# A layer of gated DeltaNet and neighbourhood attention on one core: the attention's values read from the normed values without a copy, one lasting slot for the wide weights, value stores issued by ScalarE, and one norm segment in another bank

## The chip, the cores and the metric

The kernel runs on one core of a Trainium2 chip. The core has a matrix engine (TensorE, PE in the profile, with PEld for its weight loads), VectorE (DVE), ScalarE (ACT), GpSimd (POOL) and SyncE (SP), which here issues transfers only. The engines run side by side and wait for each other by semaphores. Transfers are carried by 16 DMA engines; an engine's queue issues them in order, and an instruction that waits holds everything behind it in the queue of its engine. The metric is the time of one execution on the device in microseconds; the comparison is between medians of runs.

## What is computed

One layer of a hybrid transformer on 1024 latent tokens (16 rows of 64) and 256 context tokens, model width 1024, all in float32. The reference, cut to what matters here:

```python
px = modulate(rms_norm(x, norm1_w[i]), sh1, sc1) @ w_in[i]
pc = modulate(rms_norm(ctx, norm1_w[i]), csh1, csc1) @ w_in[i]
dn_c, s_ctx_f, s_ctx_b = gated_deltanet(pc[..., :DN_IN], ..., s_zero, s_zero)
dn_x, _, _ = gated_deltanet(px[..., :DN_IN], ..., s_ctx_f, s_ctx_b)
qx, kx, vx = na_qkv(px[..., DN_IN:], na_q_norm_w[i], na_k_norm_w[i])
qc, kc, vc = na_qkv(pc[..., DN_IN:], na_q_norm_w[i], na_k_norm_w[i])
na_x = neighborhood_attention(qx, kx, vx, kc, vc, na_rpb[i], rows)
x = x + g1 * (jnp.concatenate([dn_x, na_x], axis=-1) @ w_out[i])
x = x + g2 * swiglu(modulate(rms_norm(x, norm2_w[i]), sh2, sc2), w_ffn_in[i], w_ffn_out[i])
```

The DeltaNet has four heads of 128: a short convolution and SiLU on q, k and v, then a chunked scan (64 tokens in the reference, 128 in the kernel) in both directions, gated by z. The neighbourhood attention has eight heads of 64; a block of 16 columns sees a window of 8 rows by 32 columns, and all context keys, under one softmax with a learned bias.

## The kernel before

**Stages.** The input is normed and split into a high and a low part (hh, hl), so that each float32 product is made of three faster ones. Then comes the list `jobs`, one after the other on PE: `Block` objects of 128 columns over all 1280 tokens (kinds k, q, v of the DeltaNet, nq and nk of the attention; L408 to L562), and `Wide` objects of 256 columns of w_in (z1, nv0, nv1, z0; L564 on), made token tile by token tile. Beside the jobs run two background generators: the preparation of the scan's chunks (`block_inverses`, `preps`, which store y_d, at_d and others) and the modulation for later. Behind the jobs come the scan of ten chunks in two directions with the attention woven in, then the output projection, the second norm and the feed-forward part, which takes the span from about 918 us to the end.

**A block.** Its matmuls (L405) go to three banks named blk. `evac` copies these to cr (L453, ScalarE) and makes the convolution on VectorE (L454 to L461); `silu` is L468. `norm` (L473 on) of nq and nk multiplies the squares by a block matrix in segments (L492, over `self.segs`: two for nq, three for nk, whose context tokens come first) and takes the logarithm on ScalarE (L493). Its banks come from `bank()`, which gives the bank named m unless another name is passed; the preparations use one named pr. `finish` (L520 on) transposes the result of k and v to token order and stores it; v's tile vt is made by VectorE (L531) and stored to v_d by SP (L535).

**A wide job.** `prefetch` (L576) loads two halves of its weights as wraw (L586; one raw buffer for both), ScalarE makes the high part of zw (L587) and POOL the low part (L588). `tiles` multiplies (L595). The slot for zw comes from the pool zp for z1, nv0 and nv1. This pool lies in the group `late`, which is closed two jobs before the end, when `block_inverses` and `preps` have been drained; z0 then gets a slot in a new pool sp1, which the scan later uses again for its output oacc.

**The attention** (`attention`, L254) works in 32 pairs of heads by quarter of the columns and half of the rows. A pair loads two bias tiles bt (L272) and its values vw (L278); scores (L303) go to sc, VectorE adds the bias and takes the maximum (L305, mx), ScalarE the exponential (L307), VectorE the division (L309, bt); PE transposes (L314), ScalarE copies (L317, pt), and PE multiplies by vc and vw (L324). The generator is stepped from z0's token tiles (`next(fill)` from the fourth tile on) and then from the scan. Before the last job, `next(fill)` issues the loads of the first pair: qs, kh, kl, vc, bt and vw. A load of vw reads one piece of 128 x 384 from vw_d, a copy of the latent part of nv_d in window order, which 64 transfers of SP write after nv1 (L1104 to L1109).

**The scan** (`load`, L1161, and `scan`, L1188) reads v, kt, y, kT, qT and at of a chunk with SP (L1165) into three buffers of each kind and multiplies at L1198, L1208, L1217, L1229 and L1234.

**What sets the order.** Except in one passage that is marked as ordered by hand, the layer that builds the program orders the instructions of each engine by its own rules, from the dependences, the pools and the program's text. So a changed line moves instructions that it does not name, and the order of SP's queue is not that of the text. A slot that a closed pool leaves to a new one carries the waits of its former users. In the order's rows the names DMAHW0 to DMAHW7 are eight semaphores of transfers which the program uses in turn.

Of the kernel before, what the change touches and what calls it, by code (L numbers as in the profile page):

```python
# [9 lines left out]
F32 = mybir.dt.float32  # L10
F32R = mybir.dt.float32r
# [8 lines left out]
D, L, CT, T = 1024, 1024, 256, 1280  # L20
KT = 8
# [7 lines left out]
BLKS = [0, 8, 24, 32]  # L29
# [59 lines left out]
def hybrid(ctx, tc, a, dbg):  # L89
# [26 lines left out]
    def const(name, shape, dt=F32):  # L116
        return mid.tile(shape, dt, name=name, tag=name)
# [17 lines left out]
        dve.memset(bias[:, i:i + 1], v)  # L135
    b_eps, b_naq = bias[:, 0:1], bias[:, 1:2]
    mr = const("mr", [128, 5, 128], F32R)
    mneg = const("mneg", [128, 2, 128], F32R)

    v_d = dram.tile([T, 512], F32, name="v_d", tag="v_d")  # L140
    k_d = dram.tile([T, 512], F32, name="k_d", tag="k_d")
# [8 lines left out]
    vw_d = dram.tile([128, 4, 4, 4, 128], F32, name="vw_d", tag="vw_d")  # L150
# [103 lines left out]
    def attention(nw):  # L254
# [20 lines left out]

        def values(hp, half, cb):
            vw = nw.tile([128, 3, 128], F32, name="vw", tag="vw", bufs=3)
            sp.dma_start(vw, vw_d[:, hp, cb, half:half + 3])  # L278
            return vw

        def context(hp):
# [93 lines left out]
    with ExitStack() as bs:  # L375
# [32 lines left out]
        class Block:  # L408
# [64 lines left out]
            def norm(self):  # L473

                kind, acc, t0, i = self.kind, self.acc, self.t0, self.i
                if kind == "v":
                    return
                if kind == "k":
                    sp.dma_start(kT_d[:, :, i], acc.rearrange("p (c t) -> p c t", t=128))
                    return  # L480
                r = self.r
                if kind == "q":
                    sp.dma_start(qT_d[:, :, i], acc[:, t0:].rearrange("p (c t) -> p c t", t=128))
                    p = bank()
                    for c in range(8):
                        pe.matmul(p[:, c:c + 1], r[:, t0 + c * 128:t0 + (c + 1) * 128], M[C_ONE][:, 0:1],
                                  start=True, stop=True)
                    dve.tensor_copy(SQ[:, :, i], p[:, 0:8])
                    return
                for s0, n in self.segs:  # L490
                    p = bank()
                    pe.matmul(p[:, :n], M[C_BD2], r[:, s0:s0 + n], start=True, stop=True)  # L492
                    act.activation(r[:, s0:s0 + n], p[:, :n], AF.Ln, bias=b_eps, scale=1.0 / ND)  # L493
                if kind == "nq":
                    act.activation(r[:, t0:], r[:, t0:], AF.Exp, scale=-0.5, bias=b_naq)
                else:
                    act.activation(r[:, t0:], r[:, t0:], AF.Exp, scale=-0.5)
                isk = kind == "nk"
                u = acc
                dve.scalar_tensor_tensor(u[:, t0:], u[:, t0:], qkw[:, isk:isk + 1], r[:, t0:],  # L500
                                         op0=OP.mult, op1=OP.mult)
                hl16 = cp.tile([128, 2, T], F16, name="hl16", tag="kx", bufs=3)
                h16, l16 = hl16[:, 0], hl16[:, 1]
                if isk:
                    act.copy(h16, u)
                    dve.tensor_tensor(l16, u, h16, OP.subtract)
                else:
                    for hf in range(2):
                        s = slice(t0 + hf * 512, t0 + hf * 512 + 512)
                        uv = u[:, s].rearrange("p (r b c) -> p b r c", r=8, b=4)  # L510
                        hv, lv = (x[:, s].rearrange("p (b r c) -> p b r c", b=4, r=8) for x in (h16, l16))
                        act.copy(hv, uv)
                        dve.tensor_tensor(lv, uv, hv, OP.subtract)
                for i, x in enumerate((h16, l16)):
                    for hb in range(2):
                        hd = 2 * self.i + hb
                        dst = nk_d[i, hd] if isk else nq_d[hd, i]
                        sp.dma_start(dst, x[hb * 64:hb * 64 + 64, t0:])

            def finish(self):  # L520
                kind, acc, i = self.kind, self.acc, self.i
                if kind in "kv":
                    vt = cp.tile([128, NCH, 128], F32, name="vt", tag="kx", bufs=3)
                    for g, m in ((0, 4), (4, 4), (8, 2)):
                        p = bank()
                        for c in range(m):
                            pe.transpose(p[:, c * 128:(c + 1) * 128], acc[:, (g + c) * 128:(g + c + 1) * 128], ident)
                        if kind == "k":
                            act.copy(vt[:, g:g + m].rearrange("p c d -> p (c d)"), p[:, :m * 128])
# [5 lines left out]
                    sp.dma_start(dst[:, i * 128:(i + 1) * 128].rearrange("(c p) d -> p c d", p=128), vt)  # L535
# [28 lines left out]
        class Wide:  # L564


            def __init__(self, kind, half, zp):
                self.kind, self.half, self.zp = kind, half, zp
                self.n = 272 if kind == "z" and half else 256
                self.lasting = kind == "z" and not half  # L570

            def room(self):
                w = self.zp().tile([128, 2, KT, 256 if self.lasting else 272], F32R, name="zw", tag="zw")
                self.hi, self.lo = w[:, 0], w[:, 1]

            def prefetch(self):  # L576
                h2, n = 2 * self.half, self.n // 2
                src = a["w_nv"] if self.kind == "nv" else a["w_z%d" % self.half]
                if self.kind == "z":
                    h2 = 0  # L580
                if not self.lasting:
                    self.room()
                for i in range(2):
                    raw = wp.tile([128, KT, 136], F32, name="wraw", tag="wraw", bufs=1)
                    r, s = raw[:, :, :n], slice(i * n, i * n + n)
                    sp.dma_start(r, src[h2 + i])  # L586
                    act.copy(self.hi[:, :, s], r)  # L587
                    pool.tensor_tensor(self.lo[:, :, s], r, self.hi[:, :, s].bitcast(F32), OP.subtract)  # L588
# [55 lines left out]
        with ExitStack() as xs:  # L644
# [65 lines left out]
            with tc.manual_schedule(engines={mybir.EngineType.PE, mybir.EngineType.DVE, mybir.EngineType.Activation}):  # L710
# [30 lines left out]
                for k in range(1, KT):  # L741
# [11 lines left out]
                                ada(q, act.copy)  # L753
                    if k == 5:
                        act.copy(mr[:, 4], ident)
                        for d in range(2):
                            act.mul(mneg[:, d], masks[:, d], -1.0e30)
                        act.copy(mr[:, 0:4], masks)

        cp = pools(bs, "cp", "right")  # L760
        late = ExitStack()
        adp = pools(late, "adp", "left")
        zpool = [pools(late, "zp", "left")]
        first_half = ExitStack()
# [4 lines left out]
        def zp():  # L769
            return zpool[0]  # L770

        def decay_tables(gp):
            def small(name):
# [253 lines left out]
                        yield  # L1027
                flush(tick[0] + 2)

        jobs = first + [Block("k", 2), Block("k", 3), Wide("z", 1, zp)]  # L1030
        inv = len(jobs)
        jobs += [Block("nk", i) for i in range(3)] + [Wide("nv", 0, zp), Block("nk", 3)]
# [4 lines left out]
        jobs += [Block("nq", i) for i in range(4)] + [Block("v", 0), Wide("nv", 1, zp)]  # L1037
        values = len(jobs) - 1
        jobs += [Block("v", i) for i in (1, 2, 3)] + [Wide("z", 0, zp)]

        def blk(n):
            return jobs[n] if 0 <= n < len(jobs) and isinstance(jobs[n], Block) else None
# [9 lines left out]
        for n in range(2, len(jobs) + 2):  # L1052
# [47 lines left out]
            for _ in fin:  # L1100
                pass
            done.add(n - 2)
            if isinstance(j, Wide) and n == values:
                vlat = nv_d[CT:].rearrange("(r c) d -> r c d", c=64)  # L1104
                for cb in range(4):
                    for ch in range(4):
                        for r in range(4):
                            sp.dma_start(vw_d[r * 32:r * 32 + 32, :, cb, ch],
                                         vlat[4 * ch + r, BLKS[cb]:BLKS[cb] + 32].rearrange("c (h d) -> c h d", d=128))  # L1109
            if nrm:  # L1110
                nrm.norm()
            if isinstance(j, Block):
# [401 lines left out]
    with ExitStack() as us:  # L1514
# [66 lines left out]
        w = {}  # L1581
# [196 lines left out]
```

## Time and profile before

| | us |
|---|---|
| median of 3 runs | 1549.68 |
| lowest, highest | 1549.65, 1550.4 |
| the profiled execution | 1549.54 |
| its span | 1547.5 |
| PE busy | 1479.8 |
| VectorE busy | 994.3 |
| ScalarE busy | 727.7 |

The mean granted clock of the profiled execution is 0.982. The page gives busy time by engine, the span in 40 slices and the chain of work that ended last; the rows shown with the prediction come from it, from the list of waits, from windows (busy time of each engine in a stretch, then the granted clock, the share of the DMA engines and GB/s) and from timelines. A line number in a row is that of the kernel before.

### The profile page before, as it was taken

To read this page: it belongs to the slowest core of one execution; us is meant where nothing else is said; L and a number is where in the kernel's file an instruction comes from. 1 tells how busy PE (TensorE), PEld (TensorE's weight loads), DVE (VectorE), ACT (ScalarE), POOL (GpSimd) and SP (SyncE) were. 2 spreads that over 40 slices of the span, in tenths; PEclk is the share of its full clock that TensorE was granted. 3 is DMA by queue.
4 is the path that set the end of the run, shared out by engine and by line. 5 is a ranking of instruction groups with operands and counts; after the bars stand their busy time and mean duration, and the time that the engine had idled before them with its cause. 6 is when DMAs were issued, how large, how long until landed. Compare 5 with 4: busy or idle time off the path is not lost. (4 is left out here: it accounts for less than half of the span.)

```text
span 1547.5 us, 23963 instructions
## 1 busy us (share of the span) xinstructions
PE 1479.8 (96%) x8702; PEld 1235.2 (80%) x8702; DVE 994.3 (64%) x1712; ACT 727.7 (47%) x1404; POOL 233.6 (15%) x286
## 2 busy tenths in 40 slices
PE   6999999899989978999999999999999999999998
PEld 3788787678778867888887878888888888888887
DVE  5774497675554543777986469866665556599652
ACT  5442552635764235666773166333333334354440
POOL 1154500733554010111210000000000000000000
PEclk9999999999999979999999999999999999999999
DMA  9274221577556467899637502632323324698742
GB/s 389 64 217 133 67 72 63 163 212 241 182 169 212 130 174 237 283 288 261 220 102 255 208 34 82 211 102 103 103 102 103 109 100 159 231 381 279 244 144 82
DMA packets 204118, 267.35 MB, mean 173 GB/s; under 512 B 16736, under 2 KB 114528, under 8 KB 202976
## 3 DMA queue, kind: packets, MB, share of 16 engines
q1 hardware_dynamic: 198480, 261.07, 51.7%
q10 hardware_dynamic: 5520, 4.76, 0.9%
q8 instruction: 68, 1.11, 0.3%
q14 instruction: 50, 0.41, 0.1%
HBM read 201.02 MB, written 68.94 MB: 174 GB/s over the span
## 5 line engine op out<-in xcount | busy, mean ns | idle before, releaser
L405 PE MATMUL blk<-hh,whi 128*128 128x512 f32 (+1 forms) x410 | 123.4, 395 | 2.3 <-ACT kk L550 1.4
L1415 ACT CAST uhi<-wq 128x512 fp32r<-128x512 f32 x101 | 61.0, 622 | 133.5 <-issue 84.6
L1415 ACT CAST uhi<-ws 128x512 fp32r<-128x512 f32 x91 | 53.9, 621 | 147.3 <-PE ps L1354 92.9
L405 PE MATMUL blk<-hl,whi 128*128 128x512 f32 (+1 forms) x410 | 116.8, 377 | 0.3 <-DVE hl L707 0.3
L595 PE MATMUL blk<-zw,hh 128*128 128x256 f32 (+1 forms) x576 | 115.0, 293 | 1.3 <-ACT kk L550 1.1
L405 PE MATMUL blk<-hh,wlo 128*128 128x512 f32 (+1 forms) x410 | 114.7, 377 | 0.6 <-POOL wlo L200 0.6
L1416 DVE TENSOR_TENSOR ulo<-wq,uhi 128x512 fp32r<-128x512 f32 x101 | 67.4, 687 | 59.1 <-ACT uhi L1415 34.0
L1354 PE MATMUL ps<-hT,uhi 128*128 128x512 f32 x336 | 103.7, 390 | 0.0
L1354 PE MATMUL ps<-hT,ulo 128*128 128x512 f32 x336 | 103.5, 389 | 0.0
L1354 PE MATMUL ps<-lT,uhi 128*128 128x512 f32 x336 | 103.4, 389 | 0.0
L595 PEld LDWEIGHTS blk<-zw,hh 128*128 128x128 f32 x576 | 92.8, 192 | 5.2 <-ACT kk L550 1.4
L1354 PE MATMUL ps<-hB,uhi 128*128 128x512 f32 x288 | 89.2, 391 | 0.6 <-ACT hB L1529 0.6
L1354 PE MATMUL ps<-lB,uhi 128*128 128x512 f32 x288 | 88.7, 389 | 0.4 <-DVE lB L1530 0.4
L1354 PE MATMUL ps<-hB,ulo 128*128 128x512 f32 x288 | 88.7, 389 | 0.0
L405 PEld LDWEIGHTS blk<-hh,wlo 128*128 128x128 f32 x410 | 72.6, 192 | 15.3 <-POOL wlo L200 0.9
L405 PEld LDWEIGHTS blk<-hl,whi 128*128 128x128 f32 x410 | 72.4, 191 | 14.5 <-DVE hl L707 0.8
L405 PEld LDWEIGHTS blk<-hh,whi 128*128 128x128 f32 x410 | 69.4, 194 | 18.2 <-issue 4.5
L595 PE MATMUL blk<-zw,hl 128*128 128x256 f32 (+1 forms) x288 | 83.2, 289 | 0.0
L1354 PEld LDWEIGHTS ps<-lT,uhi 128*128 128x128 f32 x336 | 63.1, 188 | 13.1
L1354 PEld LDWEIGHTS ps<-hT,ulo 128*128 128x128 f32 x336 | 63.1, 188 | 13.1
L1354 PEld LDWEIGHTS ps<-hT,uhi 128*128 128x128 f32 x336 | 62.9, 188 | 13.0
L200 POOL TENSOR_TENSOR wlo<-wraw,whi 128x1024 fp32r<-128x1024 f32 x18 | 44.7, 2485 | 179.2 <-ACT whi L199 160.7
(359 smaller groups left out, 3540.5 us busy)
## 6 DMA issues: line engine op xcount, KB each, us to landing
wq<-w_fo SPq DMA_DIRECT2D x99, 256.0 KB, 4.2
wq<-w_gu SPq DMA_DIRECT2D x88, 256.0 KB, 2.9
wad<-wa SPq DMA_DIRECT2D x64, 256.0 KB, 4.4
bt<-rpb SPq DMA_DIRECT2D x64, 192.0 KB, 3.8
t_d<-g SPq DMA_DIRECT2D x22, 512.0 KB, 3.6
fr<-t_d SPq DMA_DIRECT2D x44, 256.0 KB, 5.0
f_d<-g SPq DMA_DIRECT2D x33, 256.0 KB, 2.1
fr<-f_d SPq DMA_DIRECT2D x33, 256.0 KB, 3.8
```

What stands on the lines that cost most here:

```text
L200: lo_engine.tensor_tensor(o, r, h.bitcast(F32), OP.subtract)
L405: pe.matmul(o, ww[:, k], xx[k][:, s], start=k == 0 and j == 0, stop=k == KT - 1 and j == 2)
L595: pe.matmul(p[:, :c1 - c0], x[k][:, s], ww[:, k, c0:c1], start=k == 0 and j == 0, stop=k == KT - 1 and j == 2)
L1354: pe.matmul(o, w[wi][:, k], x[xi][:, k], start=first and k == 0 and j == 0, stop=k == n - 1 and j == 2, skip_group_check=True)
L1415: act.copy(hi, self.raw[key])
L1416: dve.tensor_tensor(lo, self.raw[key], hi.bitcast(F32), OP.subtract)
```

## The change

Four things change.

1. **vw_d is gone**, and with it the 64 transfers that wrote it. `values` reads from nv_d itself: four transfers for a pair, one for every fourth row of the window, 32 partitions of 3 x 128 values each, in pieces of 512 bytes.
2. **One slot for the weights of the wide jobs.** The pool sp1 is opened before `late` and holds the one slot zw for z1, nv0, nv1, z0 and later oacc. The step that opened it before the last job is gone, and so are zp and `room()` there; `prefetch` of z0 takes the slot like the others. mneg moves from the constants into the pool adp and is made from mr, after the passage ordered by hand.
3. **v's stores** to v_d go to ScalarE's queue; k's stay on SP's.
4. **The third segment** of the norm (which only nk has) takes the bank pr instead of m.

```diff
@@ mneg, in the passage ordered by hand, and the pools behind it
-    mneg = const("mneg", [128, 2, 128], F32R)
...
-                        for d in range(2):
-                            act.mul(mneg[:, d], masks[:, d], -1.0e30)
                         act.copy(mr[:, 0:4], masks)
...
         late = ExitStack()
+        sp1 = pools(middle, "sp1", "left")
         adp = pools(late, "adp", "left")
-        zpool = [pools(late, "zp", "left")]
+        mneg = adp.tile([128, 2, 128], F32R, name="mneg", tag="mneg")
+        for d in range(2):
+            act.mul(mneg[:, d], mr[:, d].bitcast(F32), -1.0e30)
@@ values
             vw = nw.tile([128, 3, 128], F32, name="vw", tag="vw", bufs=3)
-            sp.dma_start(vw, vw_d[:, hp, cb, half:half + 3])
+            for r in range(4):
+                rows = nv_d[CT:].rearrange("(n r c) d -> r c n d", r=4, c=64)[r, BLKS[cb]:BLKS[cb] + 32, half:half + 3]
+                sp.dma_start(vw[r * 32:r * 32 + 32], rows[:, :, hp * 128:hp * 128 + 128])
             return vw
@@ norm
-                for s0, n in self.segs:
-                    p = bank()
+                for j, (s0, n) in enumerate(self.segs):
+                    p = bank("pr" if j == 2 else "m")
@@ finish
-                    sp.dma_start(dst[:, i * 128:(i + 1) * 128].rearrange("(c p) d -> p c d", p=128), vt)
+                    (act if kind == "v" else sp).dma_start(dst[:, i * 128:(i + 1) * 128].rearrange("(c p) d -> p c d", p=128), vt)
@@ Wide
             def room(self):
-                w = self.zp().tile([128, 2, KT, 256 if self.lasting else 272], F32R, name="zw", tag="zw")
+                w = sp1.tile([128, 2, KT, 272], F32R, name="zw", tag="zw")
...
-                if not self.lasting:
-                    self.room()
+                self.room()
@@ the loop over the jobs
                 late.close()
-                sp1 = pools(middle, "sp1", "left")
-                zpool[0] = sp1
-                jobs[n + 1].room()
                 fill = attention(pools(attn, "nw", "left", 2))
...
-            if isinstance(j, Wide) and n == values:
-                vlat = nv_d[CT:].rearrange("(r c) d -> r c d", c=64)
-                for cb in range(4):
-                    for ch in range(4):
-                        for r in range(4):
-                            sp.dma_start(vw_d[r * 32:r * 32 + 32, :, cb, ch],
-                                         vlat[4 * ch + r, BLKS[cb]:BLKS[cb] + 32].rearrange("c (h d) -> c h d", d=128))
```

PE, VectorE and POOL have the same number of instructions in both kernels, ScalarE five more (four value stores and one table load), SP 28 more.

**SP's queue around z0's weights.** Before, the last copies into vw_d, the stores of the preparations, z0's first half, a value store, and the first of the attention's loads; z0's second half stands ten rows further down:

```order
L1108 DMA vw_d<-nv_d 128x128 x53
L1010 DMA at_d<-at 128x512 x2
L1010 DMA y_d<-y_2229 128x512
L1010 DMA y_d<-y_2230 128x512
L1010 DMA y_d<-y_2231 128x512
L1010 DMA y_d<-y_2232 128x512
L586 DMA wraw<-w_z 128x8x128
L535 DMA v_d<-vt 128x10x128
L260 DMA qs<-nq_d 128x1024
L262 DMA kh<-nk_d 64x1280
L263 DMA kl<-nk_d 64x1280
```

In the changed kernel:

```order
L1006 DMA at_d<-at 128x512 x2
L1006 DMA y_d<-y_2228 128x512
L1006 DMA y_d<-y_2229 128x512
L584 DMA wraw<-w_z 128x8x128
L1006 DMA y_d<-y_2231 128x512
L1006 DMA y_d<-y_2230 128x512
L584 DMA wraw<-w_z 128x8x128
L258 DMA qs<-nq_d 128x1024
L260 DMA kh<-nk_d 64x1280
L261 DMA kl<-nk_d 64x1280
```

Both halves of z0's weights (wraw<-w_z) now stand among the stores of y, the second directly behind the last of them; the value store is not in this queue any more, and nothing but these stands ahead of the attention's loads.

**PE at the end of the last block.** Its last matmuls (L405), the first scores (L303, with their weight loads) and z0's matmuls (of zw, L595 before, L593 in the changed kernel). Before:

```order
L405 MATMUL blk<-hh_458,wlo 128x256
L405 MATMUL blk<-hh_458,wlo 128x512 x2
L303 LDWEIGHTS qs
L303 MATMUL sc<-kh,qs 128x256
L303 LDWEIGHTS qs
L303 MATMUL sc<-kh,qs 128x256
```

In the changed kernel:

```order
L405 MATMUL blk<-hl_457,whi 128x512 x2
L405 MATMUL blk<-hh_456,wlo 128x256
L405 MATMUL blk<-hh_456,wlo 128x512 x2
L593 MATMUL blk<-zw,hh_127 128x256
L593 MATMUL blk<-zw,hl_128 128x256
L593 MATMUL blk<-zw,hh_127 128x256
```

The last block was followed by 16 matmuls of scores, two transposes, and then z0; now z0 follows directly. Three of its token tiles, 72 matmuls, and four transposes of the last block's finish (L527) stand ahead of the first scores, whose rows come further down:

```order
L593 MATMUL blk<-zw,hl_457 128x256
L593 MATMUL blk<-zw,hh_456 128x256
L527 MATMUL m<-cst,cacc 128x128 x4
L303 LDWEIGHTS qs
L303 MATMUL sc<-kh,qs 128x256
```

**SP's queue within the scan.** Here are the loads for one step of the scan, for the heads of the next pairs (qs, kh, kl) and for one pair (bt, vw), at the same place of the attention, where the last heads are loaded. Before:

```order
L1165 DMA at<-at_d 128x512
L272 DMA bt<-rpb 128x384
L260 DMA qs<-nq_d 128x1024
L262 DMA kh<-nk_d 64x1280
L1165 DMA at<-at_d 128x512
L263 DMA kl<-nk_d 64x1280
L278 DMA vw<-vw_d 128x384
L272 DMA bt<-rpb 128x384
L283 DMA vc<-nv_d 128x2x128
L262 DMA kh<-nk_d 64x1280
L272 DMA bt<-rpb 128x384
L1165 DMA kT<-kT_d 128x512
```

In the changed kernel, with L1151 for L1165:

```order
L1151 DMA qT<-qT_d 128x512
L258 DMA qs<-nq_d 128x1024
L260 DMA kh<-nk_d 64x1280
L1151 DMA at<-at_d 128x512
L1151 DMA kt<-k_d 128x512
L261 DMA kl<-nk_d 64x1280
L260 DMA kh<-nk_d 64x1280
L261 DMA kl<-nk_d 64x1280
L283 DMA vc<-nv_d 128x2x128
L270 DMA bt<-rpb 128x384 x2
L278 DMA vw<-nv_d 32x3x128 x4
L1241 DMA z<-z_d 128x512 x2
```

The scan's loads and those of the pairs alternated; now those of a step stand together, and the two biases of a pair and its four value loads behind them. From the first load of the scan to the first loads of the stage behind it the queue has 216 transfers before and 294 in the changed kernel. The next rows have, in brackets, the semaphores that the same engine's instructions wait for, a little earlier in the changed kernel:

```order
L1151 DMA at<-at_d 128x512 [waits DMAHW7_49,PE_49]
L270 DMA bt<-rpb 128x384 [waits DMAHW0_49,DVE_49,Pool_49]
L1151 DMA kt<-k_d 128x512 [waits DMAHW1_49,PE_49]
L270 DMA bt<-rpb 128x384 [waits DMAHW2_49,DVE_49,Pool_49]
L278 DMA vw<-nv_d 32x3x128 [waits DMAHW3_49]
L278 DMA vw<-nv_d 32x3x128 [waits DMAHW4_49]
L278 DMA vw<-nv_d 32x3x128 [waits DMAHW5_49]
L278 DMA vw<-nv_d 32x3x128 [waits DMAHW6_49]
L270 DMA bt<-rpb 128x384 [waits DMAHW7_49,DVE_49,Pool_49]
L270 DMA bt<-rpb 128x384 [waits DMAHW0_49,DVE_49,Pool_49]
```

Each transfer waits for the use of its semaphore eight transfers earlier, and those of bt for VectorE and POOL besides.

More of the change, by code (lines that the diff above doesn't have):

```diff
@@ L149, in hybrid @@
     nk_d = dram.tile([2, NAH, ND, T], F16, name="nk_d", tag="nk_d")
-    vw_d = dram.tile([128, 4, 4, 4, 128], F32, name="vw_d", tag="vw_d")
     y_d = dram.tile([2, NCH, 128, 4, 128], F32, name="y_d", tag="y_d")
@@ L564, in hybrid, with __init__ @@
         class Wide:
-            def __init__(self, kind, half, zp):
-                self.kind, self.half, self.zp = kind, half, zp
+            def __init__(self, kind, half):
+                self.kind, self.half = kind, half
                 self.n = 272 if kind == "z" and half else 256
-                self.lasting = kind == "z" and not half
             def room(self):
-                w = self.zp().tile([128, 2, KT, 256 if self.lasting else 272], F32R, name="zw", tag="zw")
+                w = sp1.tile([128, 2, KT, 272], F32R, name="zw", tag="zw")
                 self.hi, self.lo = w[:, 0], w[:, 1]
@@ L767, in hybrid @@
         KKc = WK[:, 1]
-        def zp():
-            return zpool[0]
         def decay_tables(gp):
@@ L1028, in preps @@
                 flush(tick[0] + 2)
-        jobs = first + [Block("k", 2), Block("k", 3), Wide("z", 1, zp)]
+        jobs = first + [Block("k", 2), Block("k", 3), Wide("z", 1)]
         inv = len(jobs)
-        jobs += [Block("nk", i) for i in range(3)] + [Wide("nv", 0, zp), Block("nk", 3)]
+        jobs += [Block("nk", i) for i in range(3)] + [Wide("nv", 0), Block("nk", 3)]
         turn = len(jobs)
@@ L1036, in hybrid @@
         queries = range(turn, later)
-        jobs += [Block("nq", i) for i in range(4)] + [Block("v", 0), Wide("nv", 1, zp)]
+        jobs += [Block("nq", i) for i in range(4)] + [Block("v", 0), Wide("nv", 1)]
         values = len(jobs) - 1
-        jobs += [Block("v", i) for i in (1, 2, 3)] + [Wide("z", 0, zp)]
+        jobs += [Block("v", i) for i in (1, 2, 3)] + [Wide("z", 0)]
         def blk(n):
```

## The prediction

> **What bounds the kernel now.** I read the page's busy table and chain first, then the waits of TensorE (PE), then windows of ten microseconds around the largest wait, and at last the timelines of SP's queue and of the engines there.
>
> The page's busy table and the head of the chain that ended last:
>
> ```profile
> PE 1479.8 (96%) x8702; PEld 1235.2 (80%) x8702; DVE 994.3 (64%) x1712; ACT 727.7 (47%) x1404; POOL 233.6 (15%) x286
> PE ps L1354 27%; PE ps L1695 14%; DVE x L1536 0%; DVE lB L1530 0%; DVE ws L1411 0%; PE ps L219 0%; DVE x L1458 0%; DVE acc L1464 0%; PE ps L1448 0%; DVE xa L1702 0%; DVEq L1411 0%
> ```
>
> PE is busy for 1479.8 of 1547.5 us, and the end of the program is matmuls of the feed-forward part, which the change leaves alone. So the change can only pay where PE stands still, or runs at a lower clock, before that part. The waits of PE (us in total, times, longest):
>
> ```profile
> PE sc L303 <- DVE mx L305: 5.7, 4, 4.1
> PE m L492 <- ACT cr L493: 5.3, 4, 1.4
> PE sc L303 <- DMA kh<-nk_d: 4.5, 1, 4.5
> PE sc L314 <- DVE bt L309: 3.4, 3, 2.3
> PE m L897 <- DVE N L891: 2.9, 1, 2.9
> ```
>
> Three of the long ones are one place. The windows give, behind the stretch's start, end and length, the busy time of PE, PEld, DVE, ACT and POOL, the granted clock, the share of the DMA engines and GB/s; below them PE's timeline of the same place, with the idle time in brackets:
>
> ```profile
> 540.00:550.00 10.00, 8.50 (x48) 6.89 (x46) 4.17 (x8) 3.15 (x5) 0.00 (x0) 1.00 0.35 104
> 550.00:560.00 10.00, 2.84 (x15) 1.81 (x16) 9.30 (x9) 1.77 (x3) 2.34 (x1) 0.62 1.07 271
> 560.00:570.00 10.00, 7.57 (x36) 6.43 (x35) 5.05 (x10) 5.39 (x9) 2.62 (x2) 0.53 0.71 217
> ```
>
> ```profile
> 553.04 0.58 PE L303 MATMUL sc<-kh,qs 128*128 128x256 f16 x2 [4.54 <-DMA kh<-nk_d]
> 559.55 0.37 PE L303 MATMUL sc<-kh,qs 128*128 128x256 f16 x1 [4.11 <-DVE mx L305]
> 563.07 0.66 PE L314 MATMUL sc<-cst,bt 128*128 128x128 f32 x2 [2.29 <-DVE bt L309]
> ```
>
> PE idles 4.54 + 4.11 + 2.29 = 10.9 us, and what it does between 550 and 570 runs at a clock of 0.62 and 0.53. At full clock 2.84 us of work would be 0.62 x 2.84, so 1.1 us shorter; 7.57 us at 0.53 would be 3.6 us shorter. This seam between the last block and z0 costs **15.6 us**. The cause stands in SP's queue:
>
> ```profile
> 495.88 36.09 SPq L1108 DMA_DIRECT2D vw_d<-nv_d  x53
> 533.18 2.42 SPq L1010 DMA_DIRECT2D y_d<-y  x4
> 535.68 0.61 SPq L586 DMA_DIRECT2D wraw<-w_z  x1
> 545.47 0.37 SPq L535 DMA_DIRECT2D v_d<-vt  x1
> 545.93 0.63 SPq L260 DMA_DIRECT2D qs<-nq_d  x1
> 555.34 0.60 SPq L586 DMA_DIRECT2D wraw<-w_z  x1
> ```
>
> Up to 532 the queue is filled with copies into vw_d. Then come the stores of y and the first half of z0's weights, then a value store that can't be issued before 545.47 because VectorE has not made its tile, and behind it, in order, all loads of the attention. z0's weights can't help PE out, since they are made only in the seam:
>
> ```profile
> 549.35 1.07 ACT L587 CAST zw<-wraw 128x1024 fp32r<-128x1024 f32 x1
> 562.05 1.03 ACT L587 CAST zw<-wraw 128x1024 fp32r<-128x1024 f32 x1
> 563.15 2.37 POOL L588 TENSOR_TENSOR zw<-wraw,zw 128x1024 fp32r<-128x1024 f32 x1 [10.31 <-ACT zw L587]
> ```
>
> **The seam after the change.** The 64 copies are gone, the value store has left SP's queue, and the slot for z0's weights is free as soon as nv1's matmuls are done. The order of the changed kernel puts z0's first weight load ahead of the last two y stores, and both casts around the activation of v's second block; on PE 72 matmuls of z0 follow the last block directly, three of its eight tiles. The rows that date it, POOL's end of the last block's weights, the landing of such a load (KB each, median us), and PE in the middle of z0:
>
> ```profile
> 517.64 2.38 POOL L200 TENSOR_TENSOR wlo<-wraw,whi 128x1024 fp32r<-128x1024 f32 x1 [17.36 <-PE pr L998]
> wraw<-w_z SPq DMA_DIRECT2D x2, 544.0 KB, 4.1
> 580.00:590.00 10.00, 10.00 (x84) 9.71 (x84) 2.27 (x5) 5.67 (x8) 0.31 (x1) 1.00 0.45 138
> ```
>
> Without the copies' 36.09 us that load is free to go near 520; with 4.1 us to land, a 1.07 us cast and a 2.37 us subtraction for each of the two halves, one after another because they share a raw buffer, the second is ready by 520 + 2 x 7.5 = 535, before PE's last block ends near 548.5 (553.04 less 4.54). The attention's loads, some 0.6 us each, start behind it and are landed long before PE comes to them three tiles later: 72 matmuls, at 10 us for 84, are 8.6 us. By then VectorE is also through with the convolution that fills its 9.30 us of 550 to 560, and with it the wait for mx is gone. What stays: PE can't take z0's first bank before ScalarE has emptied the last block's banks, a row of the same timeline:
>
> ```profile
> 548.13 1.35 ACT L453 COPY cr<-blk 128x256 f32<-128x256 f32 x3 [5.77 <-PE blk L405]
> ```
>
> That is 1.0 us of waiting. I add 1.0 us for the first scores, whose biases still go through VectorE and ScalarE. The bounds are 0.4 (the banks alone, partly hidden) and 4.4 (the whole of the former wait for VectorE comes back beside the small ones). So the seam gives 15.6 - 2.0 = **13.6 us**, between 11.2 and 15.2. The two casts now stand in front of evacuations of a block; a cast that waits for its load holds them. The evacuation at 548.13 came 5.77 us after ScalarE had run dry, so one cast fits. Between 0 and 2.6 us (two casts and part of a landing) I take **+0.5**.
>
> **The norm segment.** Only the four nk blocks have a third segment. Its bank was the one in which the first segment's result waited for ScalarE: 5.3 us in four waits. In the other bank it doesn't wait for that, but it shares this bank with the chunk preparations, and VectorE sets the pace around three of the four:
>
> ```profile
> 197.00:253.00 56.00, 53.37 (x353) 47.43 (x352) 53.80 (x51) 23.93 (x34) 5.12 (x2) 1.00 0.20 57
> ```
>
> VectorE is busy for 53.80 of 56 us there, and the 2.9 us wait of L897 for it stands in the list above: time won ahead of it is in part waited out at it. Bounds 0 and -5.3; I take **-2.5**.
>
> **The value stores.** Four issues of about 0.4 us each (0.37 above) move to ScalarE, busy 47%: nothing on PE. The last one stands behind two exponentials there, and the scan's first loads wait for it. The order also puts one more attention pair without scan work beside it before the first scan matmul. Such a pair, alone, shows these waits now:
>
> ```profile
> 597.54 0.27 PE L303 MATMUL sc<-kh,qs 128*128 128x256 f16 x1 [1.02 <-DVE mx L305]
> 598.62 0.77 PE L314 MATMUL sc<-cst,bt 128*128 128x128 f32 x5 [0.38 <-ACT pt L317]
> 600.17 0.48 PE L324 MATMUL sc<-pt,vc 128*64 128x128 f32 x1 [0.78 <-ACT pt L317]
> ```
>
> Their sum is 2.2 us; I take **+2**, between -1 (the next pair then has company) and +5 (two pairs, and the granted clock falls with the gaps as it did in the seam).
>
> **The pair's values.** One load becomes four, 32 become 128. From a pair to the next there are (794.7 - 554.8) / 31 = 7.7 us by the first of these rows:
>
> ```profile
> L278 SPq DMA_DIRECT2D vw<-vw_d x32: 319/326/786, 554.8 to 794.7; - x32
> SPq L278 <- PE sc L324: 24.0, 20, 2.8
> SPq L272 <- PE sc L314: 22.9, 33, 1.8
> bt<-rpb SPq DMA_DIRECT2D x64, 192.0 KB, 3.8
> L305 DVE CUSTOM_DVE_ANT_0 bt<-sc,bt x16: 808/825/825, 761.4 to 805.5; 128x640 f32<-128x640 f32 x16
> 640.00:680.00 40.00, 39.90 (x376) 35.37 (x373) 28.70 (x83) 27.67 (x76) 4.95 (x12) 1.00 0.92 283
> 680.00:720.00 40.00, 39.60 (x372) 35.29 (x371) 28.92 (x84) 24.93 (x66) 5.69 (x13) 1.00 0.98 275
> ```
>
> Three more issues at the median of 0.326 us are 1.0 us of SP per pair, 2.4 at the longest, 0.786. The two rows of waits are SP's own from 605 to 815: 47 us for PE to free bias and value buffers, 1.7 us for each of the 27 pairs that 210 us hold, so the median fits. But the order now lists the scan's loads of a step in a batch, then the biases and values of two pairs; a scan load that waits for the step before holds the biases behind it. By an estimate, counting PE's work along the order from the last such release to a bias's first use, half of the biases have 10 us or more now, and had 12.6; at two or three places it is 4 us, less than the 0.3 + 3.8 + 0.8 us from a bias's issue over its landing to VectorE's result. Each of these costs a microsecond or so: **+2**, between 0 and +8 (three places at the longest of the former waits, 2.8).
>
> The engines' own time hardly grows. From 499.78 on the queue issued 47 of the 64-KB copies in 32.18 us, in the same pieces of 512 bytes, at a share of 0.33 of the DMA engines:
>
> ```profile
> 499.78 32.18 SPq L1108 DMA_DIRECT2D vw_d<-nv_d  x47
> 520.00:530.00 10.00, 10.00 (x58) 8.21 (x57) 8.00 (x11) 3.03 (x3) 0.02 (x1) 1.00 0.33 93
> ```
>
> So 64 KB take 32.18 / 47 x 0.33 = 0.23 us of all engines, four times 48 KB 0.69 us; at the 283 GB/s for a share of 0.92 one load of 192 KB takes 0.64 us. The Trainium skill speaks against the split: DMA: Bandwidth & Descriptors, section Bandwidth, calls transfers under 64 KB descriptor-dominated and lists 0.95 us for 64 KB against 6.15 us for 1 MB. An estimate from that page would be 3.5 us for four against 1.7 us for one, 1.8 us more for each pair. The trace's 0.23 us for 64 KB speaks against it, as far as transfers that overlap can.
>
> **The rest.** The copies' removal frees SP while PE is busy throughout (10.00 of 10.00 in 520 to 530): nothing. Two products of ScalarE for mneg move to a later place beside PE's blocks; three larger copies took 1.35 us above, so nothing, at worst +1.
>
> **The sum**, against the profiled execution (1549.54 us, of which the span is 1547.5; the median of the runs is 1549.68): -13.6 + 0.5 - 2.5 + 2 + 2 = -11.6, so **1538 us**. With every term at its better end it would be 1528, with every term at its worse end 1555.
>
> **Rivals.** (1) The seam's gain comes back at the end of z0. After the scores come later, the pairs that z0 used to carry are fewer or later, and PE waits for VectorE and ScalarE between 585 and 610 instead; the rows at 597 to 600 speak for it, the 72 matmuls moved ahead of the scores against it, since the same pairs stand within z0 as before. If two thirds of the gain go that way, 1538 + 9 = **1547 us**, between 1543 and 1550. That z0's weights are not ready in time belongs here: SP, ScalarE and POOL would each have to slip by 8 us.
>
> (2) **Slower**: the scan's queue. By the order SP hands its transfers to eight completion semaphores in turn, and each waits for the one eight places before. From the first scan load (602) to 800 the order has 216 transfers before and 294 after. That is 0.92 us for each before and 0.67 after. Eight in flight that land after 3.8 us give 0.48 us each, so it holds; if four more small ones in a row push the landing beyond 5.4 us, SP sets the pace. At 0.75 us each the stretch is 294 x 0.75 = 220 us instead of 198, +22, less the other terms' 13.6: 1549.5 - 13.6 + 22 = **1558 us**. It is slower than before by what can be told from 0.73 us on ((13.6 + 3.1) / 294 above 0.67). For it speaks the DMA share of 0.92 to 0.98; against it SP's waits for buffers, which are slack.
>
> (3) **Slower**: small transfers occupy the DMA engines for a fixed time each. If it was the engines and not the queue that spaced the copies, one cost 32.18 / 47 = 0.68 us, and four for a pair 2.7 us, 2.1 more than one load of 192 KB. From 640 to 720 the engines have 3.2 + 0.8 = 4.0 us left; 10.4 pairs would ask for 22. The 18 us that are missing are waited out at the scan's loads: 1538 + 18 = **1556 us**. A share of 0.33 during the copies speaks against it. With the 1.8 us estimated from the Trainium skill (DMA: Bandwidth & Descriptors, section Bandwidth) it would be 15 us, 1553.
>
> **How the numbers follow.** Forecast 0.62, rival (1) 0.17, rival (2) 0.15, rival (3) 0.06. A measurement of this kernel tells a change from none beyond about 0.2%, 3.1 us. The forecast is faster; of (1) three fifths are faster and two fifths the same; (2) and (3) are slower. So faster 0.72, same 0.07, slower 0.21. The range holds the forecast's bounds and (1), 1530 to 1553; what is left out is mostly (2) and (3), which reach from 1553 to 1570.
>
> **What would show it.** Right: no copy into vw_d; both casts of zw before 540; z0's first matmul within 2 us of the last block's; PE above 9.5 of 10 with a clock of 1.00 in all windows from 540 to 580; L492's wait down from four to one or none; the first scan matmul 10 to 13 us earlier. The forecast is wrong if PE waits for bt, v or y between 600 and 800 for more than 8 us in all, if SP shows no waits for buffers there any more, or if the blocks before 500 run more than 3 us later or earlier than now.

## The result, and the profile after

The changed kernel takes **1566.99 us** (median of 4 runs, 1564.22 to 1570.94) against 1549.66 us (4 runs): a ratio of **1.0113, with a 95% interval of 1.0086 to 1.0141**. It is slower by 17 us, where 1538 us was forecast, with a range of 1530 to 1553. The profiled execution took 1564.44 us, its span 1562.7.

Its busy times, and the chain that ended last, are almost what they were:

```profile
PE 1484.0 (95%) x8702; PEld 1237.5 (79%) x8702; DVE 998.8 (64%) x1712; ACT 729.8 (47%) x1405; POOL 234.0 (15%) x286
PE ps L1340 27%; PE ps L1681 13%; DVE x L1522 0%; DVE lB L1516 0%; DVE ws L1397 0%; PE ps L217 0%; DVE x L1444 0%; DVE acc L1450 0%; PE ps L1434 0%; DVE xa L1688 0%; DVEq L1397 0%
```

So the time went into idle PE. To find where, I use three landmarks of PE: the last block product, the last product of z0, and the first product of the output projection. Each row is one operation of one line; the two numbers after "x.. : min/median/max ns," are the start of its first and of its last instance. Before:

```profile
L405 PE MATMUL blk<-hh,wlo x410: 277/390/796, 37.0 to 548.1; 128*128 128x512 f32 x76, 128*128 128x256 f32 x61
L595 PE MATMUL blk<-zw,hh x576: 276/282/682, 107.4 to 594.9; 128*128 128x256 f32 x149, 128*128 128x272 f32 x43
L1331 PE MATMUL ps<-na,whi x32: 389/389/504, 813.7 to 824.1; 128*128 128x512 f32 x32
```

The changed kernel:

```profile
L405 PE MATMUL blk<-hh,wlo x410: 274/390/628, 35.9 to 549.9; 128*128 128x512 f32 x76, 128*128 128x256 f32 x61
L593 PE MATMUL blk<-zw,hh x576: 274/282/682, 106.6 to 581.7; 128*128 128x256 f32 x149, 128*128 128x272 f32 x43
L1317 PE MATMUL ps<-na,whi x32: 389/389/497, 829.0 to 839.3; 128*128 128x512 f32 x32
```

From the last block to the end of z0 it is 46.8 us before and **31.8 after: 15.0 won**. From the end of z0 to the output projection, the scan with the attention woven in, it is 218.8 before and **247.3 after: 28.5 lost**. The blocks end 1.8 later. That makes 829.0 - 813.7 = 15.3 us, and the span grew by 15.2. Behind that nothing moved: from the output projection to the end it is 733.8 us before and 733.7 after.

The seam looks nearly as forecast. Here are the windows of the changed kernel (columns as in the prediction). Before, PE was busy for 2.84 and 7.57 us in the last two, at a clock of 0.62 and 0.53. The 8.97 below misses the sign of 9.5 in every window, by the 1.03 us of waiting for the banks that was forecast:

```profile
540.00:550.00 10.00, 10.00 (x57) 8.40 (x55) 6.24 (x8) 1.34 (x2) 0.00 (x0) 1.00 0.82 211
550.00:560.00 10.00, 8.97 (x75) 8.67 (x74) 7.73 (x10) 3.30 (x6) 0.00 (x0) 1.00 0.57 171
560.00:570.00 10.00, 9.97 (x85) 9.35 (x83) 4.43 (x11) 5.08 (x9) 0.00 (x0) 1.00 0.31 94
```

The loss is in the scan. PE's waits there, from 598 to 830 (us in total, times, longest); from 607 to 814 before, the largest was 2.3 us and all listed ones together 5.9. The first row is that of before, the others are of the changed kernel:

```profile
PE sc L303 <- DVE mx L305: 0.5, 2, 0.3
PE sc L303 <- DVE mx L305: 8.6, 5, 5.7
PE sc L314 <- DVE bt L309: 3.1, 6, 1.0
PE sc L314 <- ACT pt L317: 2.9, 7, 0.6
PE sc L314 <- DVE mx L308: 2.5, 1, 2.5
PE sc L324 <- ACT pt L317: 2.4, 5, 1.0
PE sc L314 <- DVE mx L305: 2.4, 2, 1.4
```

All of them are steps of a pair: the maximum, the division, the copy behind it. The longest, in PE's timeline, and what SP's queue did ahead of it:

```profile
740.67 1.16 PE L1215 MATMUL ps<-vn,at 128*128 128x128 f32 x8
741.66 1.06 PE L1220 MATMUL ps<-vk,kt 128*128 128x128 f32 x8
743.11 1.11 PE L1215 MATMUL ps<-vn,at 128*128 128x128 f32 x8
744.05 1.06 PE L1220 MATMUL ps<-vk,kt 128*128 128x128 f32 x8
750.82 0.37 PE L303 MATMUL sc<-kh,qs 128*128 128x256 f16 x1 [5.71 <-DVE mx L305]
```

```profile
737.37 0.57 SPq L260 DMA_DIRECT2D kh<-nk_d  x1
741.86 0.33 SPq L1151 DMA_DIRECT2D at<-at_d  x1
742.75 0.32 SPq L1151 DMA_DIRECT2D kt<-k_d  x1
743.12 0.90 SPq L261 DMA_DIRECT2D kl<-nk_d  x1
744.07 0.59 SPq L260 DMA_DIRECT2D kh<-nk_d  x1
744.70 0.59 SPq L261 DMA_DIRECT2D kl<-nk_d  x1
745.34 0.59 SPq L283 DMA_DIRECT2D vc<-nv_d  x1
746.04 0.88 SPq L270 DMA_DIRECT2D bt<-rpb  x2
```

SP issues nothing from 737.94 to 741.86: the load of at needs a buffer that PE frees with its products L1215 of 740.67, and the load of kt one that it frees with L1220 of 741.66. The two biases stand behind five more transfers and go out at 746.04, after 3.9 us of waiting for at and 4.2 us for these five; landing takes 3.2 us in the median, and VectorE starts on the first at 749.93. PE has meanwhile run dry, and after the gap its clock is low too:

```profile
740.00:750.00 10.00, 5.11 (x52) 4.71 (x49) 6.93 (x28) 3.50 (x20) 0.00 (x0) 0.94 0.66 177
750.00:760.00 10.00, 7.81 (x43) 5.06 (x43) 5.57 (x16) 6.93 (x17) 3.39 (x4) 0.55 0.91 252
```

I paired the 64 bias loads with the 64 executions of L305 in order and took the time from landing to start. Leaving out the first ten, VectorE began within 1.5 us of the landing **2 times of 54 before and 16 times of 54 after**. This count, and the span from the end of z0 to the output projection, are the gauges of the experiments. SP's waits show what stands ahead of the late ones. Within the nine microseconds before the issue of each of the 16, SP had stood 2.7 to 5.6 us on scan loads that waited for PE. Of the other 38 that holds for 12, and their median is zero.

### The profile page after: what moved, and what is told of

Its sections match the earlier page's. It is cut to its first block, busy times and chain, and to the rows that moved or that the text cites. A ratio compares the mean times of both kernels' runs of the same rounds, so it can differ in the third digit from the quotient of the medians.

```text
span 1562.7 us, 23964 instructions
## 1 busy us (share of the span) xinstructions
PE 1484.0 (95%) x8702; PEld 1237.5 (79%) x8702; DVE 998.8 (64%) x1712; ACT 729.8 (47%) x1405; POOL 234.0 (15%) x286
## 5 line engine op out<-in xcount | busy, mean ns | idle before, releaser
L405 PE MATMUL blk<-hh,whi 128*128 128x512 f32 (+1 forms) x410 | 122.3, 391 | 4.9 <-ACT cacc L438 2.1
L405 PE MATMUL blk<-hl,whi 128*128 128x512 f32 (+1 forms) x410 | 117.1, 379 | 0.3 <-DVE hl L705 0.3
L593 PE MATMUL blk<-zw,hh 128*128 128x256 f32 (+1 forms) x576 | 113.7, 291 | 2.0 <-ACT cr L453 1.0
L405 PE MATMUL blk<-hh,wlo 128*128 128x512 f32 (+1 forms) x410 | 114.8, 376 | 0.6 <-POOL wlo L198 0.6
L593 PEld LDWEIGHTS blk<-zw,hh 128*128 128x128 f32 x576 | 91.8, 190 | 4.9 <-ACT cr L453 1.5
L405 PEld LDWEIGHTS blk<-hh,whi 128*128 128x128 f32 x410 | 69.7, 192 | 21.2 <-issue 4.0
L405 PEld LDWEIGHTS blk<-hh,wlo 128*128 128x128 f32 x410 | 72.6, 193 | 15.0 <-POOL wlo L198 0.9
L405 PEld LDWEIGHTS blk<-hl,whi 128*128 128x128 f32 x410 | 72.5, 192 | 14.4 <-DVE hl L705 0.8
L593 PE MATMUL blk<-zw,hl 128*128 128x256 f32 (+1 forms) x288 | 82.2, 286 | 0.0
L198 POOL TENSOR_TENSOR wlo<-wraw,whi 128x1024 fp32r<-128x1024 f32 x18 | 44.8, 2489 | 193.6 <-ACT whi L197 163.2
```

The lines of the kernel that those rows point to most:

```text
L198: lo_engine.tensor_tensor(o, r, h.bitcast(F32), OP.subtract)
L405: pe.matmul(o, ww[:, k], xx[k][:, s], start=k == 0 and j == 0, stop=k == KT - 1 and j == 2)
L593: pe.matmul(p[:, :c1 - c0], x[k][:, s], ww[:, k, c0:c1], start=k == 0 and j == 0, stop=k == KT - 1 and j == 2)
```

## The experiments

Landmarks as above, all in us, from one profile for each kernel. "Late" is the count just explained; the ratio is to the kernel before on the same chip.

| kernel | last block to end of z0 | end of z0 to output projection | late | ratio, 95% interval |
|---|---|---|---|---|
| before | 46.8 | 218.8 | 2 | 1 |
| changed | 31.8 | 247.3 | 16 | 1.0113, 1.0086 to 1.0141 |
| values alone | 31.9 | 244.5 | 15 | 1.0074, 1.0048 to 1.0100 |
| all but the values | 44.8 | 223.2 | 3 | 0.9994, 0.9976 to 1.0012 |
| changed, values by POOL | 31.8 | 226.4 | 6 | 0.9954, 0.9935 to 0.9972 |
| changed, at and kt by POOL | 31.8 | 226.0 | 7 | 0.9961, 0.9945 to 0.9976 |
| before, copies by POOL | 31.9 | 220.0 | 3 | 0.9914, 0.9890 to 0.9939 |
| values alone, by POOL | 31.9 | 227.9 | 9 | 0.9970, 0.9945 to 0.9994 |
| changed, values by POOL, stores by SP | 31.6 | 225.0 | 9 | 0.9964, 0.9947 to 0.9980 |
| before, copies by POOL, slot, segment | 31.7 | 221.8 | 3 | 0.9938, 0.9919 to 0.9957 |
| changed, stores by SP | 31.6 | 246.8 | 14 | 1.0110, 1.0089 to 1.0132 |

**Which part of the change slows the scan.** First the values alone on the kernel before, then everything else without them:

```diff
-            sp.dma_start(vw, vw_d[:, hp, cb, half:half + 3])
+            for r in range(4):
+                rows = nv_d[CT:].rearrange("(n r c) d -> r c n d", r=4, c=64)[r, BLKS[cb]:BLKS[cb] + 32, half:half + 3]
+                sp.dma_start(vw[r * 32:r * 32 + 32], rows[:, :, hp * 128:hp * 128 + 128])
```

> The kernel before with the first part of the change alone (no copy, four value loads on SP). The stage from the first scan product to the first product of the output projection took 206.5 us before and 230.3 us in the changed kernel. Theory A (the four loads make SP's queue come out in batches in which scan loads hold the biases), B (SP's 96 more issues) and C (small transfers occupy the DMA engines) all expect about 230 us here; the copies are gone but z0 still gets its slot late, so the total is 1565 to 1573. Theory D (another part of the change altered how pairs and scan are woven) expects 207 us and 1546 to 1550.

> The changed kernel with the first part undone (64 copies by SP, one value load for a pair). A, B and C: the scan stage is back at 205 to 209 us; the copies stand ahead of z0's first weights again, so only some of the seam's 15 us is won: 1540 to 1549. D: the scan stage stays near 230 and the total near 1567.

From the first scan product the stage took 231.1 us with the values alone, and 205.6 with all but them: theory D falls for the scan. The values alone also win the whole seam, 31.9 us, though z0's slot is the late one there: so the slot was not what held z0. The total of the first run is 1563.69 us, a little better than expected; the second has 1550.1 us and just misses the expected range, since with the copies ahead of z0's weights the seam keeps 44.8 us.

**Number, size or order.** The next two keep the changed kernel and move transfers from SP to POOL's queue, once the four value loads and once only the scan's loads of at and kt:

```diff
-                sp.dma_start(vw[r * 32:r * 32 + 32], rows[:, :, hp * 128:hp * 128 + 128])
+                pool.dma_start(vw[r * 32:r * 32 + 32], rows[:, :, hp * 128:hp * 128 + 128])
```

> The changed kernel with the four value loads issued by POOL's queue instead of SP's: as many transfers, of the same shape, but SP's queue comes out interleaved as before. A and B: scan stage 205 to 212 us, total 1540 to 1546. C: 225 to 232 us, 1562 to 1570, since the engines see the same transfers.

```diff
-                sp.dma_start(fl(t), src)
+                (pool if name in ('at', 'kt') else sp).dma_start(fl(t), src)
```

> The changed kernel with only the at and kt loads of the scan (32 transfers) issued by POOL; the four value loads stay on SP, which still issues 64 transfers more than before in this stage. A: the biases are no longer held behind a scan load that waits for PE's last step, scan stage 206 to 213, total 1541 to 1548. B: the queue is still 262 transfers long against 216, so at least half of the 24 us stays, 218 to 228 us, 1554 to 1564. C: 228 to 232, 1565 to 1570.

With the values by POOL the stage took 209.6 us and the total 1544.86: the same 128 small transfers are there, so theory C falls. With at and kt by POOL it took 208.8 us and the total 1545.0, though SP still issues all four loads of each pair: of the 28.5 us lost behind z0, 21.3 are back. Theory B, which wanted half of the loss to stay, falls, and of the four A is left. SP's waits in that run, from 602 to 799:

```profile
SPq L270 <- PE sc L314: 20.3, 30, 2.1
SPq L1151 <- PE ps L1203: 9.8, 9, 2.2
SPq L278 <- PE sc L324: 8.7, 10, 1.8
```

and in the changed kernel, from 599 to 818:

```profile
SPq L270 <- PE sc L314: 19.4, 21, 2.7
SPq L1151 <- PE ps L1215: 14.7, 5, 3.8
SPq L270 <- DVE bt L309: 11.0, 7, 3.8
SPq L1151 <- PE ps L1203: 10.8, 6, 2.8
SPq L1151 <- PE ps L1220: 9.0, 6, 3.4
```

The kernel before has the same two waits (its L1229 and L1234), shorter and more of them, from 607 to 801:

```profile
SPq L1165 <- PE ps L1229: 7.0, 11, 1.0
SPq L1165 <- PE ps L1234: 5.4, 7, 1.3
```

The waits for L1215 and L1220 in the changed kernel, 14.7 + 9.0 us in 11 pieces, are gone from SP's queue when POOL issues at and kt. POOL waits for the same products instead, 19.3 and 5.9 us, in a queue that issues no bias loads. In both of these runs the building layer also lists SP's queue interleaved again, or nearly so. So they show that the order of SP's queue costs the time, and that neither the number nor the size of the value loads does. They do not part the waits of the scan loads from the row of issues in which the biases then stand; for the waits speak the 16 late biases above.

**Is it the copies in SP's queue that made the seam?** The kernel before, with one word changed:

```diff
-                            sp.dma_start(vw_d[r * 32:r * 32 + 32, :, cb, ch],
+                            pool.dma_start(vw_d[r * 32:r * 32 + 32, :, cb, ch],
```

> The kernel before, with its 64 copies into vw_d issued by POOL's queue instead of SP's, and nothing else changed. If the copies in SP's queue were the cause of the seam, z0's weights come early here too though z0's slot and the value stores are as before: last block to end of z0 31 to 34 us (46.8 before, 31.8 in the changed kernel), the scan stage 206 us as before, end of z0 to first scan product 12 to 14 us, total 1533 to 1540 against 1549.7. If the late slot or the value store held z0, the seam stays at 44 to 47 us and the total at 1547 to 1551.

It did what the first theory said, in every number: 31.9 us for the seam, 207.1 for the stage, 12.9 from the end of z0 to the scan, 1536.82 us in all (6 runs, 1534.91 to 1542.88), against 1550.22. The copies stay, but in a queue in which none of z0's or the attention's loads waits behind them. **This version beats both kernels**, without any of the change's four parts.

It is not free. POOL's own work stands behind the copies: its last copies of y (L977) start at 520.59 us against 497.63 before, and its low part of the last block's weights (L200) at 526.08 against 517.64. In this profile the blocks end at 554.1 us against 548.1, and the granted clock from 437 to 500 is 0.95 against 1.00. Whether the copies in POOL's queue cause this or the spread between executions is not shown.

**The other parts.** Three runs looked at the value stores (the first, the second and the fourth), one at the slot and the segment:

> The kernel before with the first part of the change alone, its four value loads issued by POOL. Seam 32 us, scan stage 206 to 211 us. If ScalarE's queue for the value stores is what lengthened the way from the end of z0 to the first scan product (12.3 us before, 17.0 in the changed kernel), it is 12 to 14 us here, total 1536 to 1541; if it is the order that the missing copies give, it is 16 to 18 us, total 1540 to 1545.

> The run with the value loads by POOL, and the value stores back on SP's queue; the slot and the norm segment as in the changed kernel. End of z0 to the first scan product: 12 to 14 us if the stores' new queue costs there, 16 to 18 if it is the slot or the segment. Last block's end at 548 to 549 after the start if the stores in ScalarE's queue held its copies, 551 if it is z0's two casts. Total 1538 to 1545.

> The kernel before with the copies issued by POOL (the fastest run so far, 0.991 of before), and the lasting slot and the norm segment of the change added; the value stores stay on SP. If neither the slot nor the segment is worth anything: last block to end of z0 32 us, end of z0 to the output projection 219 to 221 us, total within 3 us of that run (1534 to 1540), L492's waits gone from the list but the first 437 us of blocks no shorter. If the slot or the segment is worth what the prediction gave the segment, 2.5 us, or more: 1530 to 1535.

> The changed kernel with the value stores back on SP's queue, all else as changed. End of z0 to the output projection: 247.3 us in the changed kernel, 244.5 with the values' part alone. If the stores' queue alone makes that difference, 243 to 246 us here, total 1560 to 1566; the biases are held by the scan's loads as before, so it stays slower than the kernel before.

With the stores on SP it is 12.7 us from the end of z0 to the first scan product in both of the first two, against 16.8 with them on ScalarE; in the fourth it is 14.0, against 17.0 in the changed kernel. But this is no loss by itself: one pair more is done before the scan, and one less within it. Taken up to the output projection, the stores make no difference (225.0 against 226.4, and 246.8 against 247.3). The first of the four missed its total (1545.57 us, expected 1536 to 1541) and its scan stage (215.1 us, expected 206 to 211). A likely cause is that the value loads wait in POOL's queue for PE to free their buffers, with POOL's clearing of the biases behind them. It is not shown: the changed kernel with its values by POOL has these waits too, 70.1 and 14.9 us, in a stage of 209.6.

```profile
POOL vw L279 <- PE sc L325: 72.4, 24, 8.7
POOL bt L270 <- PE sc L315: 16.9, 12, 4.5
```

The second missed at its other landmark, the end of the blocks: 552.2 us, with PE waiting 1.6 us for the copies cr and the stores back on SP. So the stores are not what holds these copies; z0's casts stand right ahead of them (rows in the next section). The slot and the segment added to the fastest version give 1538.88 us, within 3 us of it as expected of parts worth nothing, and 221.8 us behind z0, just above the expected 219 to 221. Each against the kernel before on its own chip, the ratios are 0.9938 and 0.9914, and their intervals overlap. The profiled execution of this version was a quick one, whose last segment of the blocks starts at 431.5 us against 439.3 in that of the fastest version; since the medians stand the other way round (1538.88 against 1536.82), whether the segment shortens the blocks by something below the spread stays open. The stores back in the changed kernel leave it at 1565.72 us.

## Why the prediction was wrong

Where the forecast went wrong can be read from the landmarks. The seam gave 15.0 us for 13.6. The blocks end 1.8 us later, where +0.5 and -2.5 made 2.0 earlier. From the end of z0 to the output projection it is 28.5 us more, for a forecast of 2 + 2: nearly all of the error is there.

**What bounds the kernel, and the seam: right.** The cause was SP's queue, the gain 15.0 us for a forecast of 13.6 within 11.2 to 15.2, and the banks' wait stayed with the 1.0 us that was read from a copy of 1.35. It is PE's only listed wait up to the end of z0; the 1.0 us added for the first scores did not come there. Only the share of the parts was unknown: the missing copies do it all, the slot nothing.

```profile
535.00 0.50 PE L405 MATMUL blk<-hh,whi 128*128 128x512 f32 x1 [1.48 <-ACT cr L453]
551.33 0.38 PE L593 MATMUL blk<-zw,hh 128*128 128x256 f32 x1 [1.03 <-ACT cr L453]
```

**The casts in front of an evacuation:** +0.5 was said, 1.48 us measured (first row above), within the bounds. The cast of 533.50 had waited 1.81 us for its load, as feared there, and the copies cr come behind it:

```profile
533.50 1.04 ACT L585 CAST zw<-wraw 128x1024 fp32r<-128x1024 f32 x1 [1.81 <-DMA wraw<-w_z]
534.57 1.35 ACT L453 COPY cr<-blk 128x256 f32<-128x256 f32 x3
```

**The norm segment: -2.5 forecast, nothing found that stands out of the spread.** L492's four waits of 5.3 us are gone. But the wait for VectorE behind them, which the prediction named, grew from 2.9 to 5.7 us, and the last segment of the blocks starts at 436.3 us against 437.7, of which 1.1 is the earlier start of the first block. The bound of zero was the right end.

```profile
PE m L893 <- DVE N L887: 5.7, 1, 5.7
```

**The value stores: +2 forecast.** The way to the first scan product is 4.7 us longer, and 3.0 of it goes when the stores are back on SP (17.0 and 14.0). The scan gives these 3.0 back: about zero. The first scan product comes 8.5 us earlier than before, where 10 to 13 were expected.

**The pair's values: this step failed.** The prediction saw the right mechanism, "a scan load that waits for the step before holds the biases behind it", and gave it +2 us, at most 8, because a count along the order found too little room only "at two or three places". The runs show 25.7 us for this part alone (244.5 - 218.8), and 16 late biases instead of two or three. Two things in that count were wrong. It took room of 10 us in PE's work for plenty, when the kernel before, with 12.6 by the same count, had 4.2 us in the median between a bias's landing and its use (3.4 in the changed kernel). The landing takes 3.8 us of the rest; the issues that stand in a row and VectorE's other work are a likely part of it, which was not measured. And it priced a late bias as one wait, when a pair is a chain: behind the late maximum, the exponential, the division and the copy come late in turn, each with a wait of its own in the list, and the clock falls around the longer gaps (0.55 above). None of the prediction's three signs of being wrong came: PE's list names the steps of the pair, and hardly the load.

**The rivals.** The first did not come: the 4.7 us between z0 and the scan are half of what it asked for, and most were given back. The second named the scan's queue, with 1558 us, and its place is right, but not its mechanism: the landing did not grow, it fell from 3.8 to 3.2 us for a bias, and SP still spent 19.4 us waiting for bias buffers. SP was not too slow; it was held. The third fell with the values by POOL. On the split that the Trainium skill speaks against (DMA: Bandwidth & Descriptors, section Bandwidth), the trace took the other side here: the four small transfers land in 2.6 us each in the median, and with them on POOL's queue the scan stage takes 209.6 us, 3.1 more than before. The 15 us that the page's estimate asks for did not come.

```profile
bt<-rpb SPq DMA_DIRECT2D x64, 192.0 KB, 3.2
vw<-nv_d SPq DMA_DIRECT2D x128, 48.0 KB, 2.6
```

What is left of the 28.5 us once the values' part is taken out is 4.4 us (all but the values, 223.2 against 218.8). It lies ahead of the scan: from the end of z0 to the first scan product that run took 17.6 us, against 12.3 before. Two runs with the slot and the segment, or with these and the stores, have it in part; whether it is the other weave of pairs and scan or the spread between executions was not tried further.

## What to carry to other kernels

In a queue that issues in order, ask of each transfer which wait stands ahead of it, before asking how many transfers there are: a load that is wanted late may wait for free, and the load behind it that is wanted soon pays. When one transfer becomes four, look at how the order around them comes out, since the layer that orders them may change it for everything in that queue. And when transfers block a queue, try another queue for them first: one word gave here what four edits did not. Ask there, too, who stands behind them.

## What was not expected of the hardware

Executions of one kernel spread more in later runs than in the first ones: the kernel before took 1549.21 to 1550.4 us in four runs beside the changed kernel, and 1543.03 to 1555.7 us in 21 runs beside the version with its copies by POOL. Differences under 3 us between kernels measured on different chips are therefore not read as such above. And 64 copies issued by POOL cost it 35 us more busy time (269.1 us against 233.6 before).
